# Thirteen of sixteen fine steps by seven products, the mask seeded by ScalarE, and a plan with two transfer queues

## The chip, the cores and the metric

The kernel runs on one core of one Trainium2 chip. The metric is the device time of one execution in microseconds (us), lower is better; the number given for a kernel is the median of several executions. One further execution is recorded by the hardware profiler, and its page and trace are what is quoted below. The engines are called as the profile calls them: PE is TensorE (PEld its weight loads), DVE is VectorE, ACT is ScalarE, POOL is GpSimd, SP is SyncE; the "q" behind a name is its sequencer, which also issues transfers.

## The reference

One layer: an RMS norm, a projection of 256 rows of 4096 numbers to 4 x 4096 columns (q, k, v and a gate), stick-breaking attention over 32 heads of 128, a gated projection back, a residual add, and a final RMS norm. All is float32.

```python
D_MODEL, SEQ, N_HEADS, HEAD_DIM = 4096, 256, 32, 128

def attn_branch(xn, w_in, w_out):
    proj = xn @ w_in                                   # 256 x 4096 @ 4096 x 16384
    q, k, v, g = jnp.split(proj, 4, axis=-1)
    o = stick_breaking_attention(to_heads(q), to_heads(k), to_heads(v))
    return (o * jax.nn.silu(g)) @ w_out                # 256 x 4096 @ 4096 x 4096

# per head: z = q k^T / sqrt(128); strictly causal mask (s < t);
# a[t,s] = exp(log_sigmoid(z[t,s]) + sum over s<j<t of log_sigmoid(-z[t,j])), 0 outside the mask; o = a v
def reference(x, norm_attn, w_in_attn, w_out_attn, ..., final_norm):
    h = x + attn_branch(rms_norm(x, norm_attn), w_in_attn, w_out_attn)
    return rms_norm(h, final_norm)
```

## The kernel before

**Units, steps, tiles.** The two big products are cut into 20 units: units 0 to 15 go through `w_in` (each makes 256 columns of each of q, k, v and gate, that is two heads), units 16 to 19 through `w_out`. A unit walks the 4096-long inner dimension in 8 steps, and each step holds 2 "fine" steps of two 128-row blocks. The code calls one step of one unit a quad: four weight tiles `raw[q, t, k]` of 128 x 1024 float32 (512 KB), t the half of the inner block, k the half of the columns. Nine `raw` buffers are shared by all (`RAW_BUFS`).

**Split operands.** Every weight tile, or sum of tiles, that PE multiplies is split: ACT rounds it to float32r (`wh`, a CAST), DVE subtracts (`wl` = tile - `wh`). One "product" is three 128x128 by 128x512 matmuls (high by high, high by low, low by high), written by `mm3`. The stationary sides `sh`, `sl` (later `oh`, `ol`) are made once, in unit 0 (and before the first `w_out` unit), for all units to use.

**Seven or eight products.** A fine step is a 2 x 2 block product. Done plainly it takes eight products; done by a Strassen-like scheme it takes seven, with sums of weight tiles as extra operands. A step whose two fine steps both take seven is in `SEVEN_IN` (`SEVEN_PARTS`, 7 parts of 128 x 1024, 14 products); a step with one of seven and one of eight is in `MIX_IN` (`MIXED_PARTS`, 6 parts, five of 128 x 1024 and one of 128 x 512, 15 products). Before, units 1 to 15 have steps 1, 3, 5, 6 in `SEVEN_IN` and 0, 2, 4, 7 in `MIX_IN`: 4 x 14 + 4 x 15 = 116 products. Unit 0 and unit 16 are plain (128 products); units 17 to 19 use `SEVEN_AFTER`, `MIX_AFTER` (119 products).

**Where the sums come from.** In a seven or mixed quad the first sum is made by a transfer: `add_block` reads the neighbouring weights again from memory and adds them into `raw[q, 1, 0]` on the fly (POOL issues it; 512 KB in a `SEVEN` quad, 256 KB in a mixed one). The other sums are DVE subtractions and additions in `sums`: three of 128 x 512 in a mixed quad, three of 128 x 1024 in a `SEVEN` quad, of which the last becomes a second adding transfer, raw into raw (`moved_third`), when the step is in `FOURTH_IN`; then two stay on DVE.

**End of a unit.** `combine` adds the seven PSUM banks b1 to b7 into q, k, v and gate rows (DVE and ACT), and `heads` follows for the two heads of the unit while PE is already in the next unit: `head` transposes q and k on PE (`tr`), ACT copies them to `qkT`, PE makes scores `z` in PSUM, DVE adds the mask tile `never` (0 or -1e30) onto the first 256 columns of `z`, ACT takes Softplus, PE adds running sums (`scan`), ACT makes the weights, PE multiplies by v, DVE multiplies by the gate (`gated`). The two heads of a unit then go to memory (`spill`) and come back as the stationary side of the `w_out` units.

**The order is written by a planner.** All of this runs inside `Plan`, a small event simulation that executes at build time: every piece of work asks an engine for a time (`work`), has a cost (`vector_ns`, `scalar_ns`, fixed numbers for PE), and a key; when the modelled engine is free, the waiting piece with the smallest key is emitted. So each engine's instruction order, which the chip follows strictly, is the order that the model found. `moved` models transfers: before, as one line of transfers for the whole core, one after the other, with 0.83 or 1.78 us per 256 KB. Constants such as `HEAD_AT`, `CAST_AHEAD`, `SUMS_AHEAD` move keys or the step at which a piece may begin. `LATE_FROM` and `LATE_BEHIND` say which parts of a seven quad PE takes only after the first parts of the next quad.

Of the kernel before, what the change touches and what calls it, by code (L numbers as in the profile page):

```python
# [19 lines left out]
P = 128  # L20
S = 256
D = 4096
H = 32
NT = S // P
KC = D // P
CW = 256
HG = CW // P
NB = D // CW
W = 2 * CW
# [11 lines left out]

SEVEN_IN, MIX_IN = (1,3,5,6),(0,2,4,7)
SEVEN_AFTER, MIX_AFTER = (1, 3, 6), (0, 2, 5)
RAW_BUFS = 9
PAIRS, LOWS = 6, 5
KEPT = 6
LAST_STEPS = (2,6,5,1,0,7,3,4)
LATE_FROM, LATE_BEHIND = 3, 1  # L50
CLOSING = "adebcf"
HEAD_AT = (3, 6)
GATE_AT = 4
HEAD_SOON, GATE_SOON = 2.0, 6.0

SPREAD = (9, 1.0)
HEADS_AHEAD = 5
HEADS_LATER = 5
AHEAD, SUMS_AHEAD = 0.5, 5.0
PIPE = 1  # L60
T3_LEAD = 2000
FOURTH_IN, FOURTH_OUT = (5, 6),()
FOURTH_AHEAD = 8.0
RAW_LEAD = 0
EARLY = 1.5
TEN_WAIT = 1500
LAST_WAIT = 1000
QK_LEAD = 1500
CAST_AHEAD = 2.0
BLOCKS_LATER = 1  # L70
NEVER = -1e30
OUT_ACT = (1, 4, 7)
# [2 lines left out]
FORM_LEAD = 0  # L75
STATS = 2, 6
AWAY, PLACE_H = (0, 1, 2), (0, 1, 0, 1, 0, 2)
EVICT = 0


PLAIN = {"C11": 1, "C21": 4, "C12": 7, "C22": 6}
# [66 lines left out]
class Plan:  # L148
# [22 lines left out]
    def __init__(self, tc):  # L171
        self.now, self.serial, self.events = 0.0, 0, []
        self.free = dict.fromkeys(self.TAIL, 0.0)
        self.waiting = {e: [] for e in self.TAIL}
        self.told, self.asleep = {}, {}
        self.rings, self.moved = {}, 0.0
        self.here = 0.0
        for name in self.TAIL:
            setattr(self, name, self.Engine(tc, getattr(tc.nc, name)))
# [63 lines left out]
            else:  # L243
                ring[1] -= 1

    def work(self, engine, cost, emit, key=None, after=None, hold=True, moves=(), wait=0):

        def request(go):  # L250
            if wait:
                self.later(self.now + wait, ready, go)
            else:
                ready(go)

        def ready(go):
            self.serial += 1
            item = (self.here if key is None else key, self.serial, cost, emit, after, go, hold, moves)
            heapq.heappush(self.waiting[engine], item)
            self.later(max(self.now, self.free[engine]), self.turn, engine)  # L260

        return request

    def turn(self, engine):
        if self.free[engine] > self.now or not self.waiting[engine]:
            return
        _, _, cost, emit, after, go, hold, moves = heapq.heappop(self.waiting[engine])
        emit()
        end = self.now + cost + (50 if engine == "scalar" and self.now > self.free[engine] else 0)
        self.free[engine] = end  # L270
        seen = end + self.TAIL[engine]
        for k, (size, adds) in enumerate(moves):
            begin = max(self.now + cost * (k + 1) / len(moves) + 1300, self.moved)
            self.moved = begin + size * (1.78e3 if adds else 0.83e3) / 2**18
            seen = self.moved + 900
        if after:
            self.later(seen, after)
        self.later(seen if hold else end, go)
        self.later(end, self.turn, engine)


# [1 line left out]
def kernel(  # L283
# [25 lines left out]
    def minus(out_, full, part):  # L309
        nc.vector.tensor_tensor(out=out_, in0=full, in1=part.bitcast(F32), op=ALU.subtract)  # L310
# [100 lines left out]
    def ten(emit, cost, last=False):  # L411
        return nc.work("tensor", cost, emit, nc.here - 1e4, wait=LAST_WAIT if last else TEN_WAIT)

    def moved(engine, emit, sizes, key, after=None, hold=False, adds=False):
        issue = 700 if engine == "gpsimd" else 330
        return nc.work(
            engine, issue * len(sizes), emit, key, after=after, hold=hold, moves=[(4 * P * n, adds) for n in sizes]
        )

    def together(*works):  # L420
        for w in works:
# [59 lines left out]
    def add_block(q):  # L481

        yield nc.until(("raw", q, 1, 0))
        w, blocks, s = quads[q][1]
        r = raw[q, 1, 0]
        n = 1 if parts[quad_parts[q][0]]["mixed"] else HALF

        def both():
            b, c = blocks
            nc.gpsimd.dma_start(  # L490
                r[:, :, 0:n, :], w[b : c + 1 : c - b, s, :, HALF : HALF + n, :].rearrange("i p k n -> p i k n"),
                accum_op=ALU.add,
            )

        yield moved(
            "gpsimd", both, [n * CW * HG], first[quad_parts[q][0]] - 2e4, after=lambda: nc.tell(("T3", q)), adds=True
        )

    def tile_done(*tile):
# [10 lines left out]
    def sums(q):  # L510
# [28 lines left out]
        def moved_third():  # L539
            yield nc.until(("lows", b))  # L540
            x, y = raw[(q, 0, 1)], raw[(q, *near)]
            yield moved(
                "gpsimd", lambda: nc.gpsimd.dma_start(x, y, accum_op=ALU.add), [HALF * W], first[g[0]] - 2e4,
                after=lambda: nc.tell(("T4", q)), adds=True,
            )
            yield nc.until(("T4", q), lead=T3_LEAD)
            nc.tell(("sums", g[0]))
            tile_done(q, 0, 1)
            tile_done(q, *near)
# [38 lines left out]
    def low(n, c):  # L588

        yield nc.until(("cast", n, c.start), *((FIRST[min(n + 3 * c.start, 2)],) if parts[n]["quad"] == 0 else ()))  # L590
        h, full = halves(wh, n, c)
        l, _ = halves(wl, n, c)
        yield dve(lambda: minus(l, full, h), (c.stop - c.start) * W, key_of(n, c))
        for k in range(c.start, c.stop):
            nc.tell(("low", n, k))
        low_done(n)
# [160 lines left out]
    for _ in range(WARM):  # L757
# [6 lines left out]
    nc.gpsimd.memset(tri_f, -1.0)  # L764
    nc.gpsimd.affine_select(
        out=tri_f, in_=tri_f, compare_op=ALU.is_ge, fill=0.0, base=0, pattern=[[-1, P]], channel_multiplier=1,
    )
    never = ap.tile([P, P], F32, name="never")
    nc.gpsimd.memset(never, 0.0)
    nc.gpsimd.affine_select(  # L770
        out=never, in_=never, compare_op=ALU.is_gt, fill=NEVER, base=0, pattern=[[1, P]], channel_multiplier=-1,
    )
    neg_tri = ap.tile([P, P], F32R, name="neg_tri")
    neg_one = neg_tri[:, 0:1].broadcast_to([P, P])
# [170 lines left out]
    def head(u, i):  # L945
# [1 line left out]
        tr = att.tile([P, 2, S], F32, tag="att", name=f"tr{u}_{i}")  # L947

        def turn():
            for k in range(2):  # L950
                for t in range(NT):
                    c = k * CW + i * P
                    nc.tensor.transpose(tr[:, k, t * P : (t + 1) * P], st["qk", u][:, t, c : c + P], ident)

        yield ten(turn, 360, last=u == NB - 1)
        if i == HG - 1:
            nc.give("one")
        qk = ap.tile([P, 2, S], F32, tag="qkh", name=f"qkT{u}_{i}")
# [2 lines left out]
        yield nc.take("att")  # L961
        z = att.tile([P, BW], F32, tag="att", name=f"z{u}_{i}")

        def scores():
            kw = dict(stop=False, skip_group_check=True)
            nc.tensor.matmul(z[:, 0:P], qk[:, 1, P:S], qk[:, 0, P:S], start=True, **kw)
            nc.tensor.matmul(z[:, P:BW], qk[:, 1, 0:P], qk[:, 0, :], start=False, **kw)

        yield ten(scores, 470, last=u == NB - 1)
        nc.give("qkh")  # L970
        yield nc.take("f")
        front = z[:, 0 : 2 * P].rearrange("p (a b) -> p a b", a=2)
        both = never.rearrange("p (a b) -> p a b", a=1).broadcast_to([P, 2, P])
        yield dve(lambda: nc.vector.tensor_tensor(out=front, in0=front, in1=both, op=ALU.add), 2 * P)

        f = ap.tile([P, BW], F32, tag="f", name=f"f{u}_{i}")

# [20 lines left out]
            nc.tensor.matmul(z[:, 2 * P : BW], neg_one, fh[:, 0:P], stop=False, **kw)  # L998
            nc.tensor.matmul(z[:, 2 * P : BW], neg_one, fl[:, 0:P], stop=True, **kw)

        yield ten(scan, 520, last=u == NB - 1)
        nc.give("qkh", "gh")
        yield nc.take("f")
        a = ap.tile([P, BW], F32, tag="f", name=f"a{u}_{i}")
# [16 lines left out]
            nc.tensor.matmul(o, v(0), a[:, P:BW], start=True, stop=False, **kw)  # L1021
            nc.tensor.matmul(o[:, P:S], v(1), a[:, 0:P], start=False, stop=True, **kw)

        yield ten(out_of_head, 575, last=u == NB - 1)
        nc.give("f")
        if i == HG - 1:
            nc.give("two")
# [4 lines left out]
    def gated_with(u, i):  # L1032
        yield nc.until(("gate", u))
        yield nc.take("att")
        both = st["both", u, i] = att.tile([P, 2, S], F32, tag="att", name=f"o{u}_{i}")
        gT = both[:, 0, :]

        def turn():
            for t in range(NT):
                nc.tensor.transpose(gT[:, t * P : (t + 1) * P], st["gv", u][:, t, CW + i * P : CW + (i + 1) * P], ident)  # L1040

        yield ten(turn, 140, last=u == NB - 1)
        if i == 0:
            yield nc.take("gh", first=True)
            st["o", u] = wp.tile([P, 4, P], F32, tag="gh", name=f"gated{u}", bufs=3)
        gated = st["gated", u, i] = st["o", u][:, 2 * i : 2 * i + 2, :].rearrange("p a b -> p (a b)")
        yield act(lambda: nc.scalar.copy(gated, gT), S)
        nc.tell(("gated", u, i))
# [425 lines left out]
```

## Time and profile before

| | us |
|---|---|
| median of 3 runs | 1715.5 (1713.85 to 1716.87) |
| the profiled execution's own time | 1713.2 |
| its span, first to last instruction | 1711.5 |
| PE busy, DVE busy, ACT busy, POOL busy | 1693.8, 1626.7, 1292.4, 229.3 |

The granted TensorE clock is 0.998 over the span. The span divides into a start of 32.4 us, unit 0 to about 124 us, units 1 to 15 with a strict period, the `w_out` units from about 1388 us, and a short end after PE's last matmul (at about 1698 us) in which the rows are scaled and written. Transfers took 61.2% of 16 engines' time in SP's queue (354.24 MB) and 27.3% in POOL's (81.15 MB). A busy engine in this table is one that has an instruction recorded as running; records of neighbouring instructions overlap at their ends, so the distance from start to start is the better price of one, and the prediction reads it from the timeline.

### The profile page before, as it was taken

The page shows a single profiled execution, that of the slowest core. Times are in us where ns is not written, and L with a number is a line of the kernel's source. Part 1 is how long each engine was busy: PE and PEld are TensorE (multiplying, and loading weights), DVE is VectorE, ACT ScalarE, POOL GpSimd, SP SyncE. Part 2 cuts the span into 40 slices and gives each one's busy share as a digit, 9 for nine tenths or more (in the row PEclk, how much of TensorE's full clock was granted, in tenths as well). Part 3 has the DMA queues.
Part 4 walks back from the last instruction along what each step waited for, and adds up shares of the span by engine and source line. Part 5 has one row for each costly group of instructions (what it writes and reads, how often), then busy time and mean ns, then how long its engine had stood idle before and what let it go on. Part 6 is the DMA issues. An engine that isn't in the chain of part 4 may idle for free.

```text
span 1711.5 us, 24638 instructions
## 1 busy us (share of the span) xinstructions
PE 1693.8 (99%) x7645; PEld 1400.9 (82%) x7645; DVE 1626.7 (95%) x1840; ACT 1292.4 (76%) x1579; POOL 229.3 (13%) x241
## 2 busy tenths in 40 slices
PE   9999999999999999999999999999999999999996
PEld 6888888888888888888888888888888888888885
DVE  7889999999999999999999999999999987999997
ACT  7968686868687878777777777777777875656564
POOL 0001111111111111111111110111011123011000
PEclk9999999999999999999999999999999999999999
DMA  9979898989898989898989798989898988798886
GB/s 322 341 213 246 249 255 250 259 251 256 249 264 238 269 232 277 230 275 228 278 231 279 226 278 227 273 234 265 240 268 244 274 268 246 231 290 259 251 249 238
DMA packets 243765, 438.82 MB, mean 256 GB/s; under 512 B 25616, under 2 KB 47888, under 8 KB 243632
## 3 DMA queue, kind: packets, MB, share of 16 engines
q1 hardware_dynamic: 196752, 354.24, 61.2%
q0 software_dynamic: 45584, 81.15, 27.3%
q10 hardware_dynamic: 1296, 1.85, 0.3%
q8 instruction: 60, 0.98, 0.3%
q14 instruction: 73, 0.60, 0.1%
HBM read 411.45 MB, written 9.96 MB: 246 GB/s over the span
## 4 chain that ended last, share of the span: by engine, by line
PE 94%; DVE 2%; DMA 2%; issue 1%; SPq 0%; ACT 0%; DVEq 0%; POOLq 0%; ACTq 0%
PE acc L167 89%; PE z L167 2%; PE o L167 2%; DMA raw<-in_w_in_dram 1%; DVE wl L167 1%; PE tr L167 1%; DMA raw<-in_w_out_dram 1%; DVE h L167 1%; DMA back<-away 0%; SPq L167 0%; DVE raw L167 0%; ACT sq L167 0%; DVE xs L167 0%; DVE back L167 0%; DVE sl L167 0%
## 5 line engine op out<-in xcount | busy, mean ns | idle before, releaser
L167 ACT CAST wh<-raw 128x1024 fp32r<-128x1024 f32 (+1 forms) x989 | 972.2, 1016 | 316.7 <-PE acc L167 137.7
L167 DVE TENSOR_TENSOR wl<-raw,wh 128x1024 fp32r<-128x1024 f32 (+1 forms) x989 | 1121.1, 1174 | 25.1 <-PE acc L167 16.9
L167 PE MATMUL acc<-wh,sh 128*128 128x512 f32 x1868 | 744.4, 399 | 0.4 <-ACT wh L167 0.4
L167 PE MATMUL acc<-wl,sh 128*128 128x512 f32 x1868 | 728.8, 390 | 0.5 <-DVE wl L167 0.4
L167 PE MATMUL acc<-wh,sl 128*128 128x512 f32 x1868 | 727.3, 389 | 1.8 <-DVE sl L167 1.8
L167 PEld LDWEIGHTS acc<-wl,sh 128*128 128x128 f32 x1868 | 350.7, 188 | 76.7 <-DVE wl L167 1.7
L167 PEld LDWEIGHTS acc<-wh,sl 128*128 128x128 f32 x1868 | 351.4, 188 | 72.1 <-DVE sl L167 3.0
L167 PEld LDWEIGHTS acc<-wh,sh 128*128 128x128 f32 x1868 | 351.1, 188 | 69.8 <-ACT wh L167 1.7
L167 DVE TENSOR_TENSOR raw<-raw,raw 128x512 f32<-128x512 f32 (+1 forms) x384 | 355.2, 928 | 2.4 <-issue 1.2
L167 POOL DMA_DIRECT2D raw<-in_w_in_dram x120 | 143.9, 1199 | 1074.6 <-DMA raw<-in_w_in_dram 730.7
L167 PE MATMUL acc<-wh,oh 128*128 128x512 f32 x485 | 189.9, 392 | 0.1
L167 PE MATMUL acc<-wl,oh 128*128 128x512 f32 x485 | 189.0, 390 | 0.0
L167 PE MATMUL acc<-wh,ol 128*128 128x512 f32 x485 | 188.7, 389 | 0.0
L167 PEld LDWEIGHTS acc<-wl,oh 128*128 128x128 f32 x485 | 91.0, 188 | 19.7 <-DVE wl L167 0.6
L167 PEld LDWEIGHTS acc<-wh,oh 128*128 128x128 f32 x485 | 91.1, 188 | 18.9 <-DVE qk_sb L167 0.4
L167 PEld LDWEIGHTS acc<-wh,ol 128*128 128x128 f32 x485 | 91.1, 188 | 18.5
L167 ACT ACT_TABLE_LOAD x80 | 102.6, 1283 | 1.4
L167 DVE TENSOR_TENSOR gv_sb<-acc,gv_sb 128x512 f32<-128x512 f32 (+1 forms) x60 | 49.1, 819 | 6.6 <-PE acc L167 6.1
L167 ACT ACTIVATE qk_sb<-qk_sb,rin_v 128x512 f32<-128x512 f32 x30 | 21.7, 724 | 28.0 <-DVE qk_sb L167 27.1
L167 POOL DMA_DIRECT2D raw<-in_w_out_dram x18 | 21.7, 1206 | 152.1 <-DMA raw<-in_w_out_dram 90.5
L167 POOL DMA_DIRECT2D raw<-raw x30 | 27.8, 925 | 42.2 <-DMA raw<-in_w_in_dram 25.2
L167 POOL DMA_DIRECT2D p<-spill x41 | 22.6, 567 | 71.4 <-DVE ol L167 37.3
(84 smaller groups left out, 657.0 us busy)
## 6 DMA issues: line engine op xcount, KB each, us to landing
raw<-in_w_in_dram SPq DMA_DIRECT2D x1022, 256.0 KB, 5.3
raw<-in_w_out_dram SPq DMA_DIRECT2D x256, 256.0 KB, 5.3
raw<-in_w_in_dram POOLq DMA_DIRECT2D x60, 512.0 KB, 7.6
raw<-in_w_in_dram POOLq DMA_DIRECT2D x60, 256.0 KB, 6.0
raw<-raw POOLq DMA_DIRECT2D x30, 512.0 KB, 7.4
p<-spill POOLq DMA_DIRECT2D x41, 128.0 KB, 4.2
raw<-in_w_out_dram POOLq DMA_DIRECT2D x9, 512.0 KB, 9.0
xr<-in_x_dram SPq DMA_DIRECT2D x16, 256.0 KB, 5.4
```

The source lines that it names most:

```text
L167: return self.tc.keep_in_program_order(getattr(self.engine, name)(*args, **kw))
```

## The change

Three things change, and the numbers that steer the order with them.

1. `SEVEN_IN`, `MIX_IN` go to (1, 3, 4, 5, 6) and (0, 2, 7): in units 1 to 15 step 4 turns from mixed to seven. Thirteen of the sixteen fine steps take seven products, 5 x 14 + 3 x 15 = 115 per unit. `FOURTH_IN` goes from (5, 6) to (3, 4, 6).
2. The mask: the tile `never` and DVE's addition of it are gone. ACT writes `neg_tri` (-1 or 0) times 1e30 into the first 256 columns of `z` before the scores, and the score matmuls add onto it (no `start`). The four transposes that use the same PSUM bank before come in another order and with `start` on the first two alone.
3. The planner: transfers are modelled as two queues (SP's and POOL's) whose front transfers share the engines packet by packet (`pour`, `arrive`, `next_landing`, `landing`), with 14 + 0.0371 r ns per packet of r bytes and 26 + 0.0742 r for an adding one. The costs of the heads' PE work grow (360 to 460, 470 to 660, 520 to 580, 575 to 665, 140 to 240 ns), and DVE's subtraction for `wl` counts as done 200 ns before its modelled end. A set of constants that move keys and earliest steps is changed with it.

```diff
-SEVEN_IN, MIX_IN = (1,3,5,6),(0,2,4,7)
+SEVEN_IN, MIX_IN = (1, 3, 4, 5, 6), (0, 2, 7)
-LATE_FROM, LATE_BEHIND = 3, 1
+LATE_FROM, LATE_BEHIND = 4, 1
-HEAD_AT = (3, 6)
-GATE_AT = 4
-HEAD_SOON, GATE_SOON = 2.0, 6.0
-SPREAD = (9, 1.0)
-HEADS_AHEAD = 5
-HEADS_LATER = 5
-AHEAD, SUMS_AHEAD = 0.5, 5.0
+HEAD_AT = (1, 6)
+GATE_AT = 3
+HEAD_SOON, GATE_SOON = 6.0, 8.0
+SPREAD = (11, 0.9)
+HEADS_AHEAD = 2
+HEADS_LATER = 8
+AHEAD, SUMS_AHEAD = 0.0, 4.0
-T3_LEAD = 2000
-FOURTH_IN, FOURTH_OUT = (5, 6),()
-FOURTH_AHEAD = 8.0
-RAW_LEAD = 0
+T3_LEAD = 1000
+FOURTH_IN, FOURTH_OUT = (3, 4, 6), ()
+FOURTH_AHEAD = 10.0
+RAW_LEAD = 300
-CAST_AHEAD = 2.0
+CAST_AHEAD = 5.0
-EVICT = 0
+EVICT = 4000
...
+    BEFORE, BEHIND = (2000, 2400), (1000, 1400)
+
+    def pour(self):
+        heads = [q[0] for q in self.queues if q]
+        if heads:
+            rounds = (self.now - self.poured) / sum(h[1] for h in heads)
+            for h in heads:
+                h[0] -= rounds
+        self.poured = self.now
...
+    def next_landing(self):
+        self.pours += 1
+        heads = [q[0] for q in self.queues if q]
+        if heads:
+            rounds = max(min(h[0] for h in heads), 0.0)
+            self.later(self.now + rounds * sum(h[1] for h in heads), self.landing, self.pours)
...
-        return nc.work(
-            engine, issue * len(sizes), emit, key, after=after, hold=hold, moves=[(4 * P * n, adds) for n in sizes]
-        )
+        moves = []
+        for n in sizes:
+            r = min(4 * n, run)
+            moves.append((P / 16 * 4 * n / r, 26 + 0.0742 * r if adds else 14 + 0.0371 * r))
...
-        yield dve(lambda: minus(l, full, h), (c.stop - c.start) * W, key_of(n, c))
+        yield dve(lambda: minus(l, full, h), (c.stop - c.start) * W, key_of(n, c), tail=-200)
...
-            for k in range(2):
-                for t in range(NT):
-                    c = k * CW + i * P
-                    nc.tensor.transpose(tr[:, k, t * P : (t + 1) * P], st["qk", u][:, t, c : c + P], ident)
+            for n, (k, t) in enumerate(((1, 0), (0, 0), (0, 1), (1, 1))):
+                c = k * CW + i * P
+                nc.tensor.matmul(
+                    tr[:, k, t * P : (t + 1) * P], st["qk", u][:, t, c : c + P], ident, start=n < 2, stop=True,
+                    is_transpose=True, skip_group_check=True,
+                )
...
+        front = z[:, 0 : 2 * P].rearrange("p (a b) -> p a b", a=2)
+        both = neg_tri.bitcast(F32).rearrange("p (a b) -> p a b", a=1).broadcast_to([P, 2, P])
+        yield act(lambda: nc.scalar.activation(front, both, AF.Copy, scale=-NEVER), 2 * P)
+
         def scores():
-            kw = dict(stop=False, skip_group_check=True)
-            nc.tensor.matmul(z[:, 0:P], qk[:, 1, P:S], qk[:, 0, P:S], start=True, **kw)
-            nc.tensor.matmul(z[:, P:BW], qk[:, 1, 0:P], qk[:, 0, :], start=False, **kw)
+            kw = dict(start=False, stop=False, skip_group_check=True)
+            nc.tensor.matmul(z[:, 0:P], qk[:, 1, P:S], qk[:, 0, P:S], **kw)
+            nc.tensor.matmul(z[:, P:BW], qk[:, 1, 0:P], qk[:, 0, :], **kw)
...
-        front = z[:, 0 : 2 * P].rearrange("p (a b) -> p a b", a=2)
-        both = never.rearrange("p (a b) -> p a b", a=1).broadcast_to([P, 2, P])
-        yield dve(lambda: nc.vector.tensor_tensor(out=front, in0=front, in1=both, op=ALU.add), 2 * P)
```

More of the change, by code (lines that the diff above doesn't have):

```diff
@@ L175, in __init__ @@
         self.told, self.asleep = {}, {}
-        self.rings, self.moved = {}, 0.0
+        self.rings = {}
+        self.queues, self.poured, self.pours = ([], []), 0.0, 0
         self.here = 0.0
@@ L244, in give, with work @@
                 ring[1] -= 1
-    def work(self, engine, cost, emit, key=None, after=None, hold=True, moves=(), wait=0):
+    def work(self, engine, cost, emit, key=None, after=None, hold=True, moves=(), wait=0, tail=None):
         def request(go):
@@ L257, in ready @@
             self.serial += 1
-            item = (self.here if key is None else key, self.serial, cost, emit, after, go, hold, moves)
+            item = (self.here if key is None else key, self.serial, cost, emit, after, go, hold, moves, tail)
             heapq.heappush(self.waiting[engine], item)
@@ L262, in work, with arrive, landing @@
         return request
+    BEFORE, BEHIND = (2000, 2400), (1000, 1400)
[6 more added lines that the diff above has]
+        self.poured = self.now
+    def arrive(self, which, job):
+        self.pour()
+        self.queues[which].append(job)
+        self.next_landing()
+    def next_landing(self):
[4 more added lines that the diff above has]
+            self.later(self.now + rounds * sum(h[1] for h in heads), self.landing, self.pours)
+    def landing(self, pour):
+        if pour != self.pours:
+            return
+        self.pour()
+        for which, q in enumerate(self.queues):
+            if q and q[0][0] < 1e-6:
+                self.later(self.now + self.BEHIND[which], q.pop(0)[2])
+        self.next_landing()
     def turn(self, engine):
@@ L266, in turn @@
             return
-        _, _, cost, emit, after, go, hold, moves = heapq.heappop(self.waiting[engine])
+        _, _, cost, emit, after, go, hold, moves, tail = heapq.heappop(self.waiting[engine])
         emit()
@@ L270, in turn, with landed @@
         self.free[engine] = end
[L271 to L276, printed above, removed]
+        seen = end + (self.TAIL[engine] if tail is None else tail)
+        if moves:
+            left = [len(moves)]
+            def landed():
+                left[0] -= 1
+                if not left[0]:
+                    if after:
+                        after()
+                    if hold:
+                        go()
+            which = engine == "gpsimd"
+            for k, (packets, ns) in enumerate(moves):
+                self.later(self.now + cost * k / len(moves) + self.BEFORE[which], self.arrive, which, [packets, ns, landed])
+        elif after:
             self.later(seen, after)
-        self.later(seen if hold else end, go)
+        if not (moves and hold):
+            self.later(seen if hold else end, go)
         self.later(end, self.turn, engine)
@@ L412, in ten, with moved @@
         return nc.work("tensor", cost, emit, nc.here - 1e4, wait=LAST_WAIT if last else TEN_WAIT)
-    def moved(engine, emit, sizes, key, after=None, hold=False, adds=False):
+    def moved(engine, emit, sizes, key, after=None, hold=False, adds=False, run=2048):
         issue = 700 if engine == "gpsimd" else 330
-        return nc.work(
-            engine, issue * len(sizes), emit, key, after=after, hold=hold, moves=[(4 * P * n, adds) for n in sizes]
-        )
+        moves = []
+        for n in sizes:
+            r = min(4 * n, run)
+            moves.append((P / 16 * 4 * n / r, 26 + 0.0742 * r if adds else 14 + 0.0371 * r))
+        return nc.work(engine, issue * len(sizes), emit, key, after=after, hold=hold, moves=moves)
     def together(*works):
@@ L495, in add_block @@
         yield moved(
-            "gpsimd", both, [n * CW * HG], first[quad_parts[q][0]] - 2e4, after=lambda: nc.tell(("T3", q)), adds=True
+            "gpsimd", both, [n * CW * HG], first[quad_parts[q][0]] - 2e4, after=lambda: nc.tell(("T3", q)), adds=True,
+            run=4 * n * CW,
         )
@@ L543, in moved_third @@
                 "gpsimd", lambda: nc.gpsimd.dma_start(x, y, accum_op=ALU.add), [HALF * W], first[g[0]] - 2e4,
-                after=lambda: nc.tell(("T4", q)), adds=True,
+                after=lambda: nc.tell(("T4", q)), adds=True, run=4096,
             )
@@ L767 @@
     )
[L768 to L772, printed above, removed]
     neg_tri = ap.tile([P, P], F32R, name="neg_tri")
@@ L949, in turn @@
         def turn():
-            for k in range(2):
-                for t in range(NT):
-                    c = k * CW + i * P
-                    nc.tensor.transpose(tr[:, k, t * P : (t + 1) * P], st["qk", u][:, t, c : c + P], ident)
-        yield ten(turn, 360, last=u == NB - 1)
+            for n, (k, t) in enumerate(((1, 0), (0, 0), (0, 1), (1, 1))):
[4 more added lines that the diff above has]
+                )
+        yield ten(turn, 460, last=u == NB - 1)
         if i == HG - 1:
@@ L962, in head @@
         z = att.tile([P, BW], F32, tag="att", name=f"z{u}_{i}")
+        front = z[:, 0 : 2 * P].rearrange("p (a b) -> p a b", a=2)
+        both = neg_tri.bitcast(F32).rearrange("p (a b) -> p a b", a=1).broadcast_to([P, 2, P])
+        yield act(lambda: nc.scalar.activation(front, both, AF.Copy, scale=-NEVER), 2 * P)
         def scores():
-            kw = dict(stop=False, skip_group_check=True)
-            nc.tensor.matmul(z[:, 0:P], qk[:, 1, P:S], qk[:, 0, P:S], start=True, **kw)
-            nc.tensor.matmul(z[:, P:BW], qk[:, 1, 0:P], qk[:, 0, :], start=False, **kw)
-        yield ten(scores, 470, last=u == NB - 1)
+            kw = dict(start=False, stop=False, skip_group_check=True)
+            nc.tensor.matmul(z[:, 0:P], qk[:, 1, P:S], qk[:, 0, P:S], **kw)
+            nc.tensor.matmul(z[:, P:BW], qk[:, 1, 0:P], qk[:, 0, :], **kw)
+        yield ten(scores, 660, last=u == NB - 1)
         nc.give("qkh")
         yield nc.take("f")
-        front = z[:, 0 : 2 * P].rearrange("p (a b) -> p a b", a=2)
-        both = never.rearrange("p (a b) -> p a b", a=1).broadcast_to([P, 2, P])
-        yield dve(lambda: nc.vector.tensor_tensor(out=front, in0=front, in1=both, op=ALU.add), 2 * P)
         f = ap.tile([P, BW], F32, tag="f", name=f"f{u}_{i}")
@@ L999, in scan @@
             nc.tensor.matmul(z[:, 2 * P : BW], neg_one, fl[:, 0:P], stop=True, **kw)
-        yield ten(scan, 520, last=u == NB - 1)
+        yield ten(scan, 580, last=u == NB - 1)
         nc.give("qkh", "gh")
@@ L1022, in out_of_head @@
             nc.tensor.matmul(o[:, P:S], v(1), a[:, 0:P], start=False, stop=True, **kw)
-        yield ten(out_of_head, 575, last=u == NB - 1)
+        yield ten(out_of_head, 665, last=u == NB - 1)
         nc.give("f")
@@ L1040, in turn @@
                 nc.tensor.transpose(gT[:, t * P : (t + 1) * P], st["gv", u][:, t, CW + i * P : CW + (i + 1) * P], ident)
-        yield ten(turn, 140, last=u == NB - 1)
+        yield ten(turn, 240, last=u == NB - 1)
         if i == 0:
```

## The prediction

> **What bounds the kernel now.** I read four views: the page's first lines, the chain of waits in order of time, the busy time by stretches, and the groups of instructions inside one unit. The page says that PE is busy nearly always, which by itself proves nothing, since matmul records overlap.
>
> ```profile
> span 1711.5 us, 24638 instructions
> PE 1693.8 (99%) x7645; PEld 1400.9 (82%) x7645; DVE 1626.7 (95%) x1840; ACT 1292.4 (76%) x1579; POOL 229.3 (13%) x241
> ```
>
> The chain that ended last (start, length, what) is the better proof. Inside units 1 to 15 it never leaves PE, and it repeats:
>
> ```profile
> 629.67 2.77 PE acc L167 x12
> ...
> 676.08 37.43 PE acc L167 x165
> 713.52 0.44 PE tr L167 x4
> 713.95 2.77 PE acc L167 x12
> 716.73 0.66 PE z L167 x4
> 717.38 8.19 PE acc L167 x36
> ...
> 759.71 0.65 PE o L167 x4
> ```
>
> Here 165 matmuls follow each other in 37.43 us: 0.2268 us from start to start, a product of three 0.6805 us. The 12-matmul piece that began at 629.67 begins again at 713.95: a unit lasts 84.28 us. Its 348 matmuls of products take 78.9; the other 5.3 belong to its two heads. The stretches (length, then busy time of PE, PEld, DVE, ACT, POOL, the clock, the share of the transfer engines, GB/s) show unit 0, such a unit, two parts of it, and the end:
>
> ```profile
> 32.40:124.00 91.60, 91.58 (x406) 75.91 (x407) 78.43 (x129) 74.77 (x130) 6.16 (x5) 1.00 0.88 285
> 629.67:713.95 84.28, 84.28 (x386) 70.00 (x385) 82.43 (x87) 66.29 (x76) 11.99 (x11) 1.00 0.92 251
> 666.00:676.00 10.00, 10.00 (x49) 8.36 (x48) 9.20 (x10) 9.09 (x11) 1.20 (x1) 1.00 1.02 286
> 676.00:686.00 10.00, 10.00 (x46) 8.26 (x46) 9.35 (x12) 5.92 (x7) 1.78 (x2) 1.00 1.00 307
> 1560.00:1645.00 85.00, 85.00 (x377) 70.41 (x376) 81.53 (x86) 52.90 (x61) 8.95 (x8) 1.00 0.87 263
> 1645.00:1711.50 66.50, 52.91 (x234) 43.50 (x232) 56.69 (x82) 36.30 (x56) 1.20 (x1) 0.94 0.72 239
> ```
>
> So PE bounds every unit, but DVE is busy 82.43 of 84.28 us and the transfer engines 92%. Three resources stand within 8% of each other; the change takes from the first and gives to the other two. That is the whole question.
>
> **What the change takes from PE.** Step 4 of units 1 to 15 makes 14 products instead of 15: 15 x 3 = 45 matmuls less, 45 x 0.2268 = **10.2 us**, 0.68 a unit, so PE needs 83.60 us a unit. The heads keep their matmuls: four transposes, two scores, four scans, and so on, only in another order or with another start flag; I cost that at nothing, and the count of interruptions (about 0.05 us each beyond their own length, 2.77 against 12 x 0.2268) stays five a head.
>
> **What it gives to DVE.** The groups of one unit (busy, mean ns of one) and the timeline of DVE there:
>
> ```profile
> L167 DVE TENSOR_TENSOR wl<-raw,wh 128x1024 fp32r<-128x1024 f32 x48 | 56.5, 1215 | 0.0
> L167 DVE TENSOR_TENSOR raw<-raw,raw 128x1024 f32<-128x1024 f32 x10 | 12.1, 1214 | 0.0
> L167 DVE TENSOR_TENSOR wl<-raw,wh 128x512 fp32r<-128x512 f32 x4 | 2.7, 681 | 0.0
> 633.78 0.42 DVE L167 TENSOR_TENSOR z<-z,never 128x256 f32<-128x256 f32 x1
> 634.12 1.21 DVE L167 TENSOR_TENSOR wl<-raw,wh 128x1024 fp32r<-128x1024 f32 x1
> 635.25 1.21 DVE L167 TENSOR_TENSOR raw<-raw,raw 128x1024 f32<-128x1024 f32 x1
> 658.35 0.43 DVE L167 TENSOR_TENSOR z<-z,never 128x256 f32<-128x256 f32 x1 [0.36 <-PE z L167]
> 676.19 0.42 DVE L167 TENSOR_TENSOR gated<-o,gated 128x256 f32<-128x256 f32 x1 [0.99 <-PE o L167]
> 682.27 1.42 DVE L167 TENSOR_TENSOR gv_sb<-acc,gv_sb 128x512 f32<-128x512 f32 x2 [0.39 <-PE acc L167]
> 690.54 0.68 DVE L167 TENSOR_TENSOR gv_sb<-acc,gv_sb 128x512 f32<-128x512 f32 x1
> 691.14 0.68 DVE L167 TENSOR_TENSOR raw<-raw,raw 128x512 f32<-128x512 f32 x1
> ```
>
> From start to start a 1024-wide subtraction costs 1.13 us, a 512-wide one 0.60, the mask 0.34; the records are 0.08 longer. Per unit after the change: `wl` goes from 48 wide and 4 narrow to 50 and 3 (7 parts for 6); the sums on DVE go from 10 wide (two steps with three, two with two) and 12 narrow to 12 wide (two with three, three with two, as `FOURTH_IN` takes one from each of three steps) and 9 narrow; two masks go. Net 4 x 1.13 - 4 x 0.60 - 2 x 0.34 = **+1.44 us**.
>
> DVE's idle time in the unit is 84.28 - 82.43 = 1.85, and 1.74 of it is the three waits shown, all for PE: DVE came early. A wait that vanishes also lets the record before it overlap, 3 x 0.08. So DVE needs 82.43 + 0.11 - 0.24 + 1.44 = **83.74 us** a unit without any wait, against PE's 83.60. DVE becomes the slower by 0.14 a unit, 2.1 us over 15 units, if its waits vanish. They can, because they are slack; they need not, because DVE works strictly in the written order and a gate or eviction placed too early still holds every `wl` behind it. The plan now charges the heads 2.605 us of PE each where it charged 2.065; the trace has 5.3 / 2 = 2.67, so the order should ask for PE's results nearer to when they come. Against the 2.1 us stands the lead that DVE carries into unit 1 (78.43 busy of 91.60 us in unit 0): at most five `wl` tiles of 1.36 us each, at least nothing. I take half of 2.1 as lost.
>
> **The other terms, costed at nothing.** ACT gets two wide casts for one narrow one and two mask seeds a unit.
>
> ```profile
> L167 ACT CAST wh<-raw 128x1024 fp32r<-128x1024 f32 x48 | 48.8, 1049 | 12.3 <-PE acc L167 5.5 <-DMA raw<-in_w_in_dram 3.1 <-DVE raw L167 3.0
> L167 ACT CAST sh<-xs 128x256 fp32r<-128x256 f32 x4 | 1.6, 398 | 1.3 <-DVE xs L167 1.3
> L167 ACT ACTIVATE a<-z 128x384 f32<-128x384 f32 x32 | 15.5, 486 | 4.7 <-PE z L167 4.6
> ```
>
> No row shows ACT writing 256 columns from SBUF into PSUM; between nothing and the 0.49 of a 384-wide one, nearest the 0.40 of a 256-wide cast. 2 x 1.05 - 0.62 + 0.80 = +2.3 on 66.29: 82% of 83.6, covered by ACT's idle time. The seed adds a wait on PE: scores stand behind it, and behind the scores every product. Each is placed 1.5 us after the model has it ready, which covers 0.40; uncovered it would cost at most 30 x 0.49 = 15 us, and at best the lost DVE hop before Softplus gains nothing, as PE works on products meanwhile. In unit 0 one more fine step needs its seven forms, a few 128-wide subtractions, under 2.5 us on DVE, inside its 13 us of idle there. The `w_out` units keep their products, and PE has no gap to fill in them (85.00 of 85.00); only their order changes, cost between -2 and +2 us, taken as 0. POOL issues one more transfer a unit, 0.9 us on 11.99; it stands in POOL's order ahead of the next step's first sum, and I price that with the transfers.
>
> **The sum.** -10.2 + 1.05 gives -9.1 us. Against the profiled execution's 1713.2 that is 1704.1; the median of the runs is 2.3 higher, so **1706.4** as a median. With the lead covering all of the 2.1 it is 1705.3, with none of it and 0.15 us of waits left a unit about 1709.7.
>
> **The rivals.** *The waits stay.* If DVE keeps a wait w a unit, its unit is 83.74 + w, and from w = 0.54 there is no gain at all. Gate and eviction wait 1.38 today. Half of it kept gives 84.43: +2.3 us, less 1.05 of lead, **1717**; all of it 1728. For it: both waits recur in each unit. Against it: they are DVE's slack, which is gone.
>
> *The transfers fall behind in steps 3 to 6* (the slower side).
>
> ```profile
> q1 hardware_dynamic: 9150, 16.66, 59.5%
> q0 software_dynamic: 2544, 4.46, 32.0%
> raw<-in_w_in_dram POOLq DMA_DIRECT2D x4, 512.0 KB, 7.7
> raw<-in_w_in_dram POOLq DMA_DIRECT2D x4, 256.0 KB, 6.2
> raw<-raw POOLq DMA_DIRECT2D x2, 512.0 KB, 7.8
> ```
>
> These are the queues (packets, MB, share of 16 engines) and issues of the same unit. Loads take 50.1 us of it, 6.3 a step; POOL's adding transfers 27.0 us for 4.46 MB, so 3.2 us for 512 KB and 1.6 for 256. The change adds 1.6 + 3.2: (77.1 + 4.8) / 83.6 = 98%. A `SEVEN` step with its fourth sum on the engines needs 6.3 + 3.2 + 3.2 = 12.7 us of transfers against 14 x 0.6805 = 9.5 of PE; before, two such steps stood in a row, now three of four, 3 to 6: the backlog of a unit grows from 6.3 to 9.4 us. If PE waits for more than 0.68 of those 3.1 us, the kernel is slower: for half of them, 15 x (1.55 - 0.68) = +13, **1728**; for all 1752. Moreover `LATE_FROM` lets one part less wait for the next step, so the first sum is wanted sooner. For it: the shares of 1.02 and 1.00 in the stretches above. Against it: PE lost nothing in just those, and nine `raw` buffers are over two steps, 20 us, of stock. The Trainium skill, "DMA: Bandwidth & Descriptors", "Queues, rings and completion order", has each transfer engine change round-robin between queues by packets, so that POOL's adds would slow SP's loads; the two shares agree that one pool is used up by both, no row here shows the turns.
>
> *DVE is the bound already.* Then PE's saving is worth nothing and DVE's 1.44 comes in full: 15 x 1.44 = +22, **1737**. For it: 82.43 of 84.28. Against it: all of DVE's waits in the unit are for PE, and the chain of the unit has no DVE in it. The Trainium skill, "Perfetto Trace Analysis", "Identifying the Most-Contended Engine", speaks for this rival: matmul busy time is no measure, weight loads are. By that rule PE would stand at 70.00 of 84.28, 83%, behind DVE; the even spacing of 165 matmuls says otherwise.
>
> *The end gets shorter too.* In the last stretch PE is idle for 66.50 - 52.91 = 13.6 us, after its last matmul; a better order there could give 2 us and more: 1702.
>
> **Chances.** The forecast (1704 to 1711) 0.60; waits stay 0.19, of it 0.04 under 1712; transfers 0.13; DVE bound 0.03; shorter end 0.05. A measurement of this kernel tells about 0.2%, 3.4 us. Faster by more: 0.60 + 0.05 + 0.04 = 0.69; within: 0.12 of the waits and 0.02 of the transfers, 0.14; slower 0.17. The range 1703 to 1720 takes in the forecast and the waits by half, and leaves out most of the transfers, DVE and a much shorter end, under 0.2.
>
> **What would show it.** Right: 7600 PE instructions, a period of 83.6 to 83.8 us with PE busy throughout, DVE's busy time at 83.5 or more with waits under 0.3 a unit, transfers near 97%. Wrong: PE idle in a unit released by `wl` (waits stay, or DVE), by `raw` through ACT (transfers), or ahead of `z` (the seed); any period above 84.28.

## The result and the profile after

| | before | after |
|---|---|---|
| median, us | 1715.02 (1713.81 to 1716.87, 5 runs) | 1729.24 (1725.84 to 1734.90, 5 runs) |
| the profiled execution | 1713.2 | 1734.9 |
| ratio of after to before | | 1.0083, 95% interval 1.0059 to 1.0107 |

The change makes the kernel 0.8% slower; the forecast was 1706.4, with a range that ended at 1720. The profiled execution is the slowest of the five, so its 21.7 us over before are some 7 more than the medians' 14.2. The page of after (its last two lines are transfer queues: packets, MB, time of the packets as a share of the 16 transfer engines):

```profile
span 1733.2 us, 24596 instructions
PE 1697.8 (98%) x7600; PEld 1387.4 (80%) x7600; DVE 1653.1 (95%) x1812; ACT 1314.0 (76%) x1627; POOL 240.0 (14%) x254
q1 hardware_dynamic: 196752, 354.24, 60.0%
q0 software_dynamic: 47744, 92.95, 30.1%
```

PE has the 45 instructions less, yet its busy time is longer: part of its waiting lies inside the records of matmuls. Two stretches tell where the time came from: units 1 to 15 from their first matmul to that of unit 16, then unit 16. (The marks of 124 and 1388 us that were given for the units ahead of the prediction lie some 26 us inside units 1 and 16.) The columns are length, busy time of PE, PEld, DVE, ACT, POOL with their instruction counts, clock, share of the transfer engines, GB/s. Before:

```profile
97.58:1361.93 1264.35, 1264.35 (x5762) 1050.02 (x5761) 1233.11 (x1291) 991.70 (x1143) 179.46 (x168) 1.00 0.91 252
1361.93:1454.98 93.05, 92.95 (x421) 76.58 (x420) 78.57 (x135) 64.81 (x95) 22.99 (x39) 1.00 0.83 261
```

After:

```profile
96.82:1377.36 1280.54, 1265.27 (x5717) 1037.74 (x5716) 1255.29 (x1255) 1013.78 (x1188) 190.77 (x183) 1.00 0.93 258
1377.36:1473.86 96.50, 94.56 (x421) 76.18 (x420) 79.11 (x136) 64.92 (x98) 23.08 (x40) 1.00 0.79 246
585.28:670.39 85.11, 84.22 (x382) 69.27 (x382) 84.06 (x85) 67.40 (x81) 12.76 (x12) 1.00 0.93 260
1183.83:1269.41 85.58, 84.45 (x382) 69.14 (x382) 84.05 (x85) 67.77 (x80) 12.72 (x12) 1.00 0.93 258
```

Units 1 to 15 last 16.2 us longer with 45 matmuls less (85.37 us each where 84.28 was and 83.60 forecast), unit 16 3.4 longer, what follows it 2.8 longer, and the start 0.8 shorter. Nearer to the median is the profile of a kernel further below (`EVICT` 0), whose units 2 to 15 have the same order on DVE: 1730.06 us, with units of 85.21, unit 16 at 96.18 and 0.8 us more than before behind it. In a unit, DVE is now busy 84.05 us, more than PE's whole need. The waits of the whole execution, with the total, the number of times and the longest, say who is late. After:

```profile
PE acc L167 <- DVE wl L167: 16.2, 22, 1.0
DVE wl L167 <- ACT wh L167: 21.1, 25, 2.2
```

Before:

```profile
PE acc L167 <- DVE wl L167: 0.4, 1, 0.4
DVE wl L167 <- ACT wh L167: 6.2, 10, 1.5
DVE gated L167 <- PE o L167: 13.4, 15, 1.0
```

Within units 1 to 15 alone PE waits 14.5 us for `wl` after the change, and DVE's waits for casts are 17.6 us where they were 3.3. So PE now waits for DVE, and DVE no longer for PE's results but for ACT's casts. DVE's timeline in the unit from 585.28 shows one such wait, and a detail that matters below: the sum here starts 1.25 us after the `wl` ahead of it, not 1.13. That is so at five of the 17 places of this unit where a sum stands behind a `wl`, and at one of 17 in the unit of before that the prediction reads.

```profile
643.72 1.22 DVE L167 TENSOR_TENSOR wl<-raw,wh 128x1024 fp32r<-128x1024 f32 x1
644.97 1.22 DVE L167 TENSOR_TENSOR raw<-raw,raw 128x1024 f32<-128x1024 f32 x1
649.56 4.63 DVE L167 TENSOR_TENSOR wl<-raw,wh 128x1024 fp32r<-128x1024 f32 x4 [0.77 <-ACT wh L167]
```

The longest of these waits shows what stands behind them. DVE's `wl` waits 2.22 us for a cast, and ACT had waited 4.03 us for a load of raw weights before it came to that cast. The two loads that SP issued at about 810 took 8.5 us from issue to landing, where the median of all 1022 is 5.4, and the share of the transfer engines is above 1.00. The unit lasts 86.55 us, which is little more than DVE's 84.06 us of work and this one wait:

```profile
819.67 3.89 ACT L167 CAST wh<-raw 128x1024 fp32r<-128x1024 f32 x4 [4.03 <-DMA raw<-in_w_in_dram]
821.70 2.36 DVE L167 TENSOR_TENSOR wl<-raw,wh 128x1024 fp32r<-128x1024 f32 x2 [2.22 <-ACT wh L167]
755.98:842.53 86.55, 84.75 (x382) 69.08 (x382) 84.06 (x85) 67.72 (x81) 12.73 (x12) 1.00 0.94 255
raw<-in_w_in_dram SPq DMA_DIRECT2D x2, 256.0 KB, 8.5
raw<-in_w_in_dram SPq DMA_DIRECT2D x1022, 256.0 KB, 5.4
810.00:820.00 10.00, 10.00 (x48) 8.27 (x47) 9.38 (x9) 5.44 (x8) 2.44 (x3) 1.00 1.09 255
820.00:830.00 10.00, 9.67 (x45) 7.67 (x44) 8.27 (x8) 6.94 (x8) 1.18 (x1) 1.00 1.03 315
```

Of the 17.6 us that DVE waits for casts in units 1 to 15, 13.9 us in 14 waits stand behind a row of casts that ACT could begin only when such a load had landed.

The profile alone leaves two explanations for the units: DVE has too much work, or transfers come too late. A third is the new order itself.

### The profile page after: what moved, and what is told of

The parts are those of the page before. It is cut to its first block, busy times and chain, and to the rows that moved or that the text cites. A ratio compares the mean times of both kernels' runs of the same rounds, so it can differ in the third digit from the quotient of the medians.

```text
span 1733.2 us, 24596 instructions
## 1 busy us (share of the span) xinstructions
PE 1697.8 (98%) x7600; PEld 1387.4 (80%) x7600; DVE 1653.1 (95%) x1812; ACT 1314.0 (76%) x1627; POOL 240.0 (14%) x254
## 4 chain that ended last, share of the span: by engine, by line
PE 72%; DMA 12%; DVE 10%; issue 3%; ACT 1%; SPq 1%; DVEq 0%; POOL 0%; ACTq 0%; POOLq 0%
PE acc L167 69%; DMA raw<-in_w_in_dram 9%; DVE wl L167 7%; DVE raw L167 3%; PE o L167 2%; PE z L167 2%; DMA xres<-in_x_dram 1%; ACT wh L167 1%; SPq L167 1%; DMA raw<-in_w_out_dram 1%; DMA p<-spill 1%; PE tr L167 0%; DVE h L167 0%; DMA spill<-gated 0%; DMA xr<-in_x_dram 0%
## 5 line engine op out<-in xcount | busy, mean ns | idle before, releaser
L167 ACT CAST wh<-raw 128x1024 fp32r<-128x1024 f32 (+1 forms) x1004 | 988.5, 1022 | 275.9 <-PE acc L167 114.4
L167 DVE TENSOR_TENSOR wl<-raw,wh 128x1024 fp32r<-128x1024 f32 (+1 forms) x1004 | 1146.1, 1183 | 41.7 <-ACT wh L167 21.1
L167 DVE TENSOR_TENSOR raw<-raw,raw 128x1024 f32<-128x1024 f32 (+1 forms) x369 | 360.4, 983 | 4.7 <-issue 1.6
L167 POOL DMA_DIRECT2D raw<-raw x45 | 39.8, 884 | 144.8 <-DVE wl L167 82.7
L167 ACT ACTIVATE gv_sb<-gv_sb,rin_v 128x512 f32<-128x512 f32 x30 | 21.7, 722 | 13.9 <-DVE gv_sb L167 13.8
L167 ACT CAST oh<-p 128x512 fp32r<-128x512 f32 (+3 forms) x41 | 19.4, 486 | 16.5 <-DVE p L167 11.0
```

Source lines behind the costliest of these rows:

```text
L167: return self.tc.keep_in_program_order(getattr(self.engine, name)(*args, **kw))
```

## The experiments

Times are medians; before was run beside each group (1714.67, 1714.88 and 1714.72 us).

### Less work for DVE, less for the transfers, both

Three kernels leave out half of certain sums. Every instruction of DVE and ACT keeps its place in them, so only the length of some changes.

```diff
+            part = slice(0, 1) if not mixed and parts[a]["u"] < OUT0 else slice(0, HG)
...
-                lambda: nc.vector.tensor_tensor(out=x, in0=y, in1=z, op=op), ...
+                lambda: nc.vector.tensor_tensor(out=x[:, part], in0=y[:, part], in1=z[:, part], op=op), ...
```

> The changed kernel with every instruction in the same place, but in units 1 to 15 the 1024-wide sums of raw weight tiles on DVE cover only half of the tile's columns (the other half is left unsummed): 12 x 0.53 = 6.4 us of DVE less per unit. Theory A (DVE is the bound: it needs more than PE's 83.60 us a unit, and its lead runs dry in the four seven-product steps in a row): the period falls to PE's 83.60 and the time to about 1705. Theory B (the transfers are late in steps 3 to 6, casts and DVE wait for them): the time stays at 1722 to 1732, and DVE only idles more. Theory C (the new order is worse by itself, with PE waiting where the plan puts the heads): no change either.

Measured, with half sums: 1714.23 us (1708.48 to 1717.95, 10 runs), ratio to before 0.9991 (0.9980 to 1.0002). Its profile, of the shortest of the ten runs, has the units at 83.78 us:

```profile
96.22:1352.99 1256.77, 1256.77 (x5716) 1040.10 (x5715) 1168.16 (x1255) 1007.90 (x1188) 190.79 (x183) 1.00 0.94 263
```

Theory A is right that DVE's load counts: 15 us of the change's 1729 go, and in the profiled run the units come within 0.2 us of PE's 83.60. No run reaches 1705, though, and the other nine are 3 to 9 us longer than the profiled one; no trace shows where.

```diff
+        m = 1 if parts[quad_parts[q][0]]["u"] < OUT0 else n
...
-                r[:, :, 0:n, :], w[b : c + 1 : c - b, s, :, HALF : HALF + n, :]...
+                r[:, :, 0:m, :], w[b : c + 1 : c - b, s, :, HALF : HALF + m, :]...
```

> The changed kernel with every instruction in the same place, but in units 1 to 15 the first adding transfer of a step of seven products moves 256 KB and not 512 (half of the sum is left out): about 5 x 1.6 = 8 us of the transfer engines less per unit. Theory A (DVE): the time stays within 4 us of 1729, period above 84.5. Theory B (transfers): the waits of ACT and DVE go and the period falls to about 83.8, the time to 1706 to 1710. Both at once: something between, about 1718.

Measured, with half adds: 1715.27 us (1712.75 to 1718.78, 10 runs), ratio 1.0006 (0.9996 to 1.0015). The units take 1262.60 / 15 = 84.17 us, near the 84.05 that DVE is busy in a unit of the change, and DVE's waits for casts nearly go:

```profile
95.86:1358.46 1262.60, 1261.43 (x5717) 1038.73 (x5716) 1254.26 (x1255) 1011.34 (x1187) 190.79 (x183) 1.00 0.88 247
DVE wl L167 <- ACT wh L167: 5.9, 11, 1.1
```

That was the "something between" of the expectation, lower than the 1718 put there. Three figures tie DVE's waits to the transfers. The share of the transfer engines falls from 0.93 to 0.88. DVE's idle time in units 1 to 15 falls from 25.3 us (1280.54 - 1255.29) to 8.3 (1262.60 - 1254.26), which is nearly all of the 17.9 us that these units get shorter. And the 17 loads that land just ahead of the late casts of the change take 8.1 us there as a median, while the same 17 take 6.5 us here. That loads are issued late, for want of a free `raw` buffer, is not the reason: SP's queue waits for DVE to free buffers as long in both kernels (in units 1 to 15, 421 us for `wl` and 266 for sums with the change, 423 and 270 here).

> The changed kernel with both of the earlier cuts at once: 1024-wide sums of raw tiles on DVE over half the columns, and 256 KB instead of 512 KB in the first adding transfer of a seven-product step, units 1 to 15; every instruction in its place. Theory AB (DVE has no slack left at 84.05 us busy, so the waits that late transfers cause are never made up; each relief alone left 0.2 and 0.6 us a unit): the units come to PE's 83.60, that is 25 us less than the change over units 1 to 15, and the time to 1708 to 1712, where only what the w_out units lose is left. If PE itself had become slower (a third cause), the period stays above 83.8.

Measured, with both cuts: 1708.85 us (1707.21 to 1710.43), ratio 0.9966 (0.9954 to 0.9978), inside the expectation; the units at 83.75:

```profile
96.58:1352.77 1256.19, 1256.19 (x5716) 1040.53 (x5715) 1169.07 (x1255) 1014.10 (x1188) 190.81 (x183) 1.00 0.89 248
```

This closes the sum of the units. By the medians, against this kernel the DVE load alone (half adds) costs 1715.27 - 1708.85 = 6.4 us, the transfers alone (half sums) 5.4, and both together (the change) 20.4: 8.6 us more than the sum of the two, an estimate from four medians that is good to some 5 us by their intervals. With slack on either side a stall is made up, without it each one stays. The profiled units agree for DVE (1262.60 - 1256.19 = 6.4). For the transfers they show 0.6 us (1256.77 - 1256.19), in the shortest run of half sums; where the rest of the 5.4 us lies is not shown. The saving on PE is real, too: 1264.35 - 1256.19 = 8.2 of the 10.2 us forecast, with 0.15 us a unit still lost.

### Is it the new order?

```diff
-SEVEN_IN, MIX_IN = (1, 3, 4, 5, 6), (0, 2, 7)
+SEVEN_IN, MIX_IN = (1, 3, 5, 6), (0, 2, 4, 7)
-FOURTH_IN, FOURTH_OUT = (3, 4, 6), ()
+FOURTH_IN, FOURTH_OUT = (5, 6), ()
```

> The changed kernel with the steps of before: SEVEN_IN (1, 3, 5, 6), MIX_IN (0, 2, 4, 7), FOURTH_IN (5, 6); mask, planner and constants of the change stay. Theories A and B: PE is the bound again, period 84.28, time 1713 to 1717, as before. Theory C (the new plan): slower than before, 1722 or more.

Measured: 1716.31 us, ratio 1.0008 (0.9999 to 1.0017). The new plan with the old steps keeps PE saturated, 1264.20 us for units 1 to 15:

```profile
96.05:1360.25 1264.20, 1264.20 (x5761) 1049.98 (x5760) 1228.63 (x1258) 989.62 (x1173) 177.44 (x168) 1.00 0.91 253
1360.25:1456.96 96.71, 93.36 (x421) 76.52 (x420) 76.85 (x133) 66.04 (x97) 23.07 (x39) 1.00 0.76 239
```

Its unit 16, however, lasts 96.71 us as in the change, not 93.05. So there is a loss of some 3.5 us in unit 16 that does not need the thirteenth step.

The opposite: thirteen steps and the mask by ACT under the planner and constants of before.

> The kernel before with the mask seeded by ACT and the thirteen steps (SEVEN_IN, MIX_IN and FOURTH_IN of the change), but the planner, its costs and all other constants of before. Theories A and B: slower than before, 1722 to 1740, as the load on DVE and transfers is that of the change. Theory C: 1705 to 1710, as PE's work falls by 10 us and the old order was sound.

Measured: 1788.06 us, ratio 1.0429 (1.0406 to 1.0453): far beyond what theories A and B expected. The new plan does not cause the loss in the units; it saves 59 us of what the thirteenth step would cost under the old one. One of its constants, taken back alone in the changed kernel, costs 44 us:

```diff
-LATE_FROM, LATE_BEHIND = 4, 1
+LATE_FROM, LATE_BEHIND = 3, 1
```

> The changed kernel with LATE_FROM 3 as before: the fifth part of a seven-product step waits again until PE has begun the next step, which gives its DVE sum and the first adding transfer some 1.4 us more. If the sum that is wanted sooner is what makes transfers and DVE late: period 84.3 to 84.8, time 1713 to 1722. If the load of the run of four does it, wherever the parts stand: period 85.4 or more, time 1727 or more (later parts hold their raw buffers longer).

Measured, on the changed kernel: 1773.08 us, ratio 1.0340 (1.0326 to 1.0354), units at 88.1, on the side of the second expectation. Holding the fifth part back is what hurts, not taking it early. That it keeps raw buffers occupied was argued in the expectation; no run separates it.

### The run of four, and moving load from one side to the other

```diff
-SEVEN_IN, MIX_IN = (1, 3, 4, 5, 6), (0, 2, 7)
+SEVEN_IN, MIX_IN = (0, 1, 3, 4, 6), (2, 5, 7)
-FOURTH_IN, FOURTH_OUT = (3, 4, 6), ()
+FOURTH_IN, FOURTH_OUT = (1, 4, 6), ()
```

> The changed kernel with the mixed steps at 2, 5, 7 and not 0, 2, 7 (steps of seven products at 0, 1, 3, 4, 6; fourth sums by transfer at 1, 4, 6): the same work in a unit, but no more than two seven-product steps in a row. If the run of four is what makes transfers and DVE fall behind: period 84.1 to 84.4, time 1713 to 1718. If only the total load matters, or the eviction at step 0 collides with a heavier step 0: period 85.4 or more, time 1727 or more.

Measured: 1765.64 us, ratio 1.0296 (1.0279 to 1.0314), units at 87.6. The rival's side. The waits name the place: in a unit, PE waits 0.78 us for `gv_sb` at the start of the unit and 1.8 us for a `wl` 8 us later. That is where PSUM is emptied, which this kernel puts into a step of seven products:

```profile
PE acc L167 <- DVE wl L167: 26.3, 17, 1.8
PE acc L167 <- DVE gv_sb L167: 10.9, 14, 0.8
```

Whether a run of four is bad by itself stays open, since this kernel changed where the evictions fall as well.

```diff
-FOURTH_IN, FOURTH_OUT = (3, 4, 6), ()
+FOURTH_IN, FOURTH_OUT = (1, 3, 4, 6), ()
```

> The changed kernel with FOURTH_IN (1, 3, 4, 6): one more 1024-wide sum of each unit goes from DVE (1.13 us) to an adding transfer (about 3.2 us of the transfer engines). Theory A (DVE's load weighs more): period 84.2 to 84.6, time 1712 to 1720. Theory B (transfers weigh more): period 86 or more, time 1735 or more. The same on both sides: within 4 us of 1729.

Measured: 1736.77 us, ratio 1.0125 (1.0110 to 1.0141), 7.5 us above the change, as theory B had it. The stretches do not bear out its reason: the units take 85.15 us, no more than in the change, and unit 16 is at 100.33. But this is the shortest of the kernel's four runs (1733.60 us), while the change was profiled in the longest of its five.

```profile
96.40:1373.69 1277.29, 1262.02 (x5717) 1039.38 (x5716) 1242.72 (x1240) 1015.72 (x1187) 204.43 (x198) 1.00 0.95 265
1373.69:1474.02 100.33, 96.75 (x420) 76.96 (x420) 78.78 (x136) 66.08 (x97) 23.12 (x39) 0.98 0.75 236
```

Within the units of this run one sum less on DVE and 512 KB more of adding transfers about cancel. Why unit 16 suffers, and where the other runs lose more, was not traced.

```diff
-EVICT = 4000
+EVICT = 0
```

> The changed kernel with EVICT 0 as before: the additions that empty PSUM at the end of a unit get their place 4 us later. Theory AB: no more than 3 us of change, as the load stays; if the early eviction takes DVE's time just where its lead is built up, period down to 84.6 and time to 1718; if PE needs the banks in time, slower, 1735 or more.

Measured: 1729.08 us (1726.57 to 1730.06), as the change. The traces show why this says nothing of the evictions: in units 1 to 15 DVE's order is that of the change but for one addition in unit 1, and one at the end of unit 15. The plan puts the others where they were. What the kernel gives is a second profile of the change's units, of a run nearer to the median:

```profile
96.65:1374.77 1278.12, 1264.82 (x5716) 1038.07 (x5715) 1255.18 (x1255) 1012.73 (x1185) 190.63 (x183) 1.00 0.93 259
1374.77:1470.95 96.18, 93.67 (x421) 76.46 (x420) 78.34 (x136) 66.31 (x99) 23.22 (x40) 1.00 0.79 247
```

### What unit 16 loses

The chain in unit 16 of the change runs over POOL: its adding transfer waits for a raw load and stands ahead of the reload of spilled heads, from which the stationary blocks are made.

```profile
1445.98 5.34 DMA raw<-in_w_out_dram
...
1452.36 1.19 POOL raw L167
1453.56 0.09 issue
1453.65 0.02 POOLq L167
1453.66 4.89 DMA p<-spill
...
1463.71 0.69 DVE ol L167
1464.40 0.04 issue
1464.45 5.73 PE acc L167 x24
```

```diff
-SPREAD = (11, 0.9)
-HEADS_AHEAD = 2
-HEADS_LATER = 8
+SPREAD = (9, 1.0)
+HEADS_AHEAD = 5
+HEADS_LATER = 5
```

> The changed kernel with SPREAD, HEADS_AHEAD and HEADS_LATER of before, which place the rebuilding of the stationary blocks in unit 15 and 16. Theory H (these constants make unit 16 last 96.5 us where it lasted 93.05): unit 16 falls to 93 to 94, the time by 3 to 4 us, to about 1725. Rival (EVICT, LATE_FROM or the model of transfers does it): unit 16 stays at 96 to 97, time 1727 to 1731. Units 1 to 14 unchanged, 85.4 on average.

Measured: 1730.61 us, the rival's time, but unit 16 is at 102.0, worse than either expectation. What follows it is shorter, 256.7 us, where the change has 259.3 and before 256.5. For unit 16 the new constants are the better ones; for the whole kernel the times do not tell the two apart.

```diff
-                nc.gpsimd.dma_start(y[:, 2 * k : 2 * k + 2, :], spill[2 * s + k][:, 2 * j : 2 * j + 2, :])
+                nc.sync.dma_start(y[:, 2 * k : 2 * k + 2, :], spill[2 * s + k][:, 2 * j : 2 * j + 2, :])
```

> The changed kernel with the reloads of the spilled heads (p from spill) issued by SP and not by POOL, so that they no longer stand in POOL's order behind the adding transfers of unit 16, whose issue waits for raw weights. Theory P (that queue order costs unit 16 its 3.4 us): unit 16 goes from 96.5 to 93 to 94 us, the time to 1725 or a little less; units 1 to 14 as in the change. Rival (the reloads come late because the plan asks for them late): unit 16 stays above 95.5, the time at 1727 to 1731.

Measured: 1728.39 us (1724.26 to 1732.09). Unit 16 is at 94.1, near what theory P expects, but the median hardly moves. Units 1 to 15 differ by more from run to run: DVE and ACT have the same order there as in the change, and the profiled runs take 1282.02 us here, 1280.54 in the change and 1278.12 with `EVICT` 0.

```profile
1378.34:1472.46 94.12, 93.34 (x421) 76.43 (x420) 78.17 (x136) 65.47 (x98) 4.18 (x4) 1.00 0.80 253
```

> Twelve seven-product steps under the new plan (the steps of before) with the reloads on SP's queue. Theory P: unit 16 at 93 to 94, time 1711 to 1714, a little below the kernel before, as unit 1 starts 1.5 us sooner under the new plan. Rival: unit 16 above 95.5, time 1715 to 1718.

Measured: 1712.87 us (1711.95 to 1714.33, 11 runs) beside 1714.72, ratio 0.9991 (0.9982 to 1.0000). Here the units are steady and the effect is seen, unit 16 at 92.44:

```profile
1360.42:1452.86 92.44, 92.44 (x421) 76.78 (x420) 76.92 (x133) 64.85 (x96) 4.17 (x4) 1.00 0.82 252
```

So moving the reloads to SP takes away what unit 16 loses. It does not show POOL's order as the whole cause, for two reasons. The plan also writes another order for DVE and ACT in unit 16 when the reloads stand on SP. And before, the reloads stood on POOL among adding transfers too, and PE did not wait in unit 16. The kernel is the lowest complete one of the study: twelve steps, the new plan, the mask by ACT, the reloads on SP. Its lead over before is 1.9 us with an interval that ends at 1, just at the limit of what can be told.

## Why the prediction was wrong

**PE's saving** was right: 45 matmuls, and with both reliefs the units come to 83.75 where 83.60 was forecast. The prediction held that PE was the bound before, and the runs agree: with the twelve steps under the new plan DVE has 4.5 us less to do in units 1 to 15 (1228.63 for 1233.11), and they last as long as before. The Trainium skill, "Perfetto Trace Analysis", "Identifying the Most-Contended Engine", says to judge PE's room by the use of its peak rate (MFU) and by the busy share of its weight loads, not by matmul busy time; by the weight loads PE would have had 17% of room. That share does not fit here, as the units with both reliefs come within 0.15 us of what PE's matmuls need.

**The count of DVE's work** was right (`wl` 50 and 3, sums 12 and 9), its price a little low: 83.74 us forecast, 84.05 busy and 84.17 as a period when transfers are light. Four more of a unit's sums than before start some 0.11 us late behind a `wl`, 0.44 us a unit together. That alone would have taken the forecast from 1706.4 to about 1713, counting 15 x 0.43 more.

**"If its waits vanish"** is the step that failed. The prediction let DVE run without a wait, at 83.74 us a unit. The two waits it spoke of did vanish: DVE's waits for the gate's matmul (13.4 us before) and for the eviction are no longer among its longest. Others took their place, 17.6 us in units 1 to 15 for ACT's casts, which the prediction had not priced, as before they stood at 3.3. DVE was idle 25.3 us in all there, 1.7 a unit, and 83.74 + 1.7 is the 85.4 that a unit takes. Most of these waits come from loads that land late, since half of the adding transfers takes them away. So the formula of the rival that the waits stay, 83.74 + w, was right, and its 1728 for a w of 1.38 is near the time measured, but with other waits than the two it meant.

**The transfers were a rival of their own** with 0.13, and its price for half the backlog, 1728, is the time measured. That the number agrees is luck: its mechanism was put as transfers against PE, with half of a backlog chosen, and DVE's load has no part in it. What was measured is that transfers alone cost 5.4 us and DVE alone 6.4, both together 20.4. The prediction treated two resources at 98% and 100% as separate cases with separate chances; they cost more together, because DVE can't make up a stall that a transfer causes. The load itself was put too high: 81.9 us a unit, 98% of 83.6, where 0.93 of 85.37 is 79.4. The burst above a share of 1.00, with which the prediction argued, is there after the change as well, in the two stretches shown.

**The `w_out` units** were costed at nothing, because PE had no gap in them; the plan could still open one. What unit 16 loses goes away when the reloads leave POOL's queue; why the new plan loses it and the old one did not stays open. The 2.8 us after it were not traced further.

**The rest held**, but for one point. The seed in a unit of the change (busy, mean ns):

```profile
L167 ACT ACTIVATE z<-neg_tri 128x256 f32<-128x256 f32 x2 | 0.8, 376 | 0.0
```

It costs ACT 0.376 us (0.40 taken) and PE does not wait for it in the units; `LATE_FROM` speaks for the change, not against it as the prediction had it; and what the lead into unit 1 is worth can't be seen beside losses of this size.

## What to carry to other kernels

When a change takes work from the engine that bounds and gives it to two that are over 90% busy, do not price the two one by one: what the slack of one makes up for the other is lost when neither has any, and 6.4 and 5.4 us became 20.4 here. Shorten instructions in place, one resource at a time and then both, and the parts of such a loss can be read off without changing the order. And a planned order is tied to its load: a single constant of this plan was worth 44 us with thirteen steps, while with twelve the old and the new plan run alike.

## What the runs showed of the hardware

DVE subtractions that follow one another start 1.13 us apart at 1024 columns, but some of the sums behind a `wl` started 1.25 us after it, five of 17 in a unit of the change; where DVE is the bound, four more of them are 0.44 us a unit. Adding transfers lengthen the loads beside them: the same 17 loads took 8.1 us and, with half of the first adding transfers' bytes, 6.5. The scatter of the runs also goes with the adding transfers: the runs of the change lie within 9 us and those with half sums within 9.5, those with half adds within 6, those with both within 3.2, and those of before within 4.
